# Group B's prompt attention from two streams of heads, their steps on part of the array in pairs; combine queued behind the heads

## The chip, the cores and the metric

The kernel runs on one NeuronCore of one Trainium2 chip. The metric is the device time of one execution in microseconds; the median of three runs is given, and one more execution was recorded by the profiler. Engines go by the profile's names: PE is TensorE (its weight loads are PEld), DVE VectorE, ACT ScalarE, POOL GpSimd, and SP the engine that issues most DMAs.

## What is computed

One layer of an encoder with two groups of attention heads beside each other, for a prompt of 512 frames and 8 x 16 frames of decoding, with 2048 channels in float32. The 640 frames share every projection.

```python
def prompt_layer(x, w_in, norm_mix, rel_table, sinks, norm_grp_a, norm_grp_b, w_out,
                 norm_ffn, w_gate, w_up, w_down):
    ...
    qa, ka, va, qb, kb, vb = split_proj(rmsnorm(x, norm_mix) @ w_in)
    qb = rope_partial(qb, pos)
    kb = rope_partial(kb, pos)
    ...
    oa = band_attend(qa.reshape(b, nc, CHUNK, N_HEADS_A, 1, HEAD_DIM),
                     band_gather(ka, A_PREV_CHUNKS), band_gather(va, A_PREV_CHUNKS),
                     band_valid(nc, A_PREV_CHUNKS), bias=bias)
    ob = band_attend(qb.reshape(b, nc, CHUNK, N_KV_B, GQA_R, HEAD_DIM),
                     band_gather(kb, B_PREV_CHUNKS), band_gather(vb, B_PREV_CHUNKS),
                     band_valid(nc, B_PREV_CHUNKS), sink=sinks.reshape(N_KV_B, GQA_R))
    y = merge_and_ffn(x, oa, ob, norm_grp_a, norm_grp_b, w_out, norm_ffn, w_gate, w_up, w_down)
    keep_a = min(A_REACH, s)
    keep_b = min(B_WINDOW, s)
    return y, ka[:, s - keep_a:], va[:, s - keep_a:], kb[:, s - keep_b:], vb[:, s - keep_b:]
```

`sample_layer` does the same for the decoding frames against cached keys and values. Group B has 16 query heads of 64 channels on two key and value heads, a window of its own chunk and two before, and a sink for each head.

## The kernel before

**Projections.** `dense` (L247) multiplies one tile of 128 weight columns by the 16 chunks of the input's channels. Each product of float32 is three matmuls (L235, L236, L237: high by high, high by low, low by high), for two halves of 320 frames: 16 x 2 x 3 = 96 matmuls of 128x320 a tile. The low parts come from a copy on ScalarE (L226) and a subtraction on VectorE (L227, `split`).

**Stages at the start.** First the keys and values of group B with the norm of the input. Then the eight query tiles of group B, `project_b` (two heads of one key head each; tile t), each followed by its rotation (`rope`, L555, through small DMAs) and a store of its decoding frames to the scratch tensor `sb_d` (L871). Then four tiles of group A, (1,7), (0,7), (2,6) and (2,7), each reduced by L410 or L412 and stored. Then group A's other tiles, two at a time, by a scheme with seven products instead of eight (`quartet`: p1, p6, p7, p2, p5, p4, p3; its weights are combined at L797, L801, L804 and L813, its results at L823), which needs sums of the input's chunks.

**Side work.** Attention and the sums are generators that wait in queues. A stream takes the generators of one queue in turn; `tick`, called after six projection matmuls, lets `pump` advance the next stream by one step, at a rate (`n.rate`, steps a tick). Here they are:
- `prompt_b`, one for each tile t, in the queue "heads": scores (L425) in two times two banks, masked maxima (L428), softmax (L436 to L445), four steps of transposes (L341, `flip`), and the weighing of the values (L464). Scores use 64 rows of TensorE's array (64*128 in the profile), weighings 64 columns (128*64).
- `decode_b` in "decode": loads, among them the query from `sb_d` (L584, copied at L590), then four steps of scores (L599), softmax (L612 to L616), transposes (L341) and products with the values (L651).
- `combine(k0, k1)` in "combine": for each chunk kt two loads of the input (L889, L890), sums on VectorE (L896, L903) and GpSimd (L897, L899), and three splits. Its two buffers of a chunk come from the few W buffers.

A step that uses part of the array is announced by `yield "part"`. Where two streams have such a step next, `pump` runs both (the partner's beside the first). Where no partner stands ready, a step is put off once, but before the change only with more than two streams. `drain` and `drain_queue` run what is left without projection matmuls between.

**Order and buffers.** The program is written in this order and then scheduled; `keep_pace` holds a side instruction on TensorE behind the projection matmul that it was written after. Scores, transposes and weighings share four banks of PSUM (`at`), projections two pairs (`dn`). There are 62 buffers S of 640 columns, 12 W of 1024 and some for the queries (Q). In the stage of `project_b` there was one stream of heads, and `combine(0, 3)` was queued with decode, behind the last `project_b`.

Of the kernel before, what the change touches and what calls it, by code (L numbers as in the profile page):

```python
# [49 lines left out]
class Net:  # L50
# [24 lines left out]
    def pump(self, alone=False):  # L75

        skipped = False
        for _ in range(len(self.streams)):
            name, queue = self.streams[self.turn % len(self.streams)]
            self.turn += 1  # L80
            work = self.active.get(name)
            if work is None and self.queues.get(queue):
                work = self.active[name] = self.queues[queue].pop(0)
            if work is None or work.gi_running:
                continue
            partner = None
            if self.marks.get(name) and not alone:
                partner = next((x for x, y in self.active.items() if x != name and y and self.marks.get(x)
                                and not y.gi_running), None)
                if partner is None and len(self.streams) > 2 and name not in self.waited:  # L90
                    self.waited.add(name)
                    skipped = True
                    continue
            at = self.emitted()
            self.run(name, work)
            if partner:
                self.run(partner, self.active[partner])
                self.due -= 1
            self.side.append((at, self.emitted()))
            return True  # L100
        return skipped and self.pump(alone)
# [218 lines left out]
def build(nc, tc, io, pools):  # L320
    n = Net(nc, tc, io, pools)
# [24 lines left out]
    def pack(t, k):  # L346
        v = r(sh(t, 2, k))
        return v[:, 0], v[:, 1]
# [56 lines left out]
    def proj(idx, lst, ps=None, gain=None):  # L405
        if ps is None:
            ps = n.dense([(io["w_in"][idx, :, k:k + 8], 8) for k in (0, 8)], acts)
        out = n.get(lst)
        if gain is None:
            nc.vector.tensor_tensor(halves(out[:, :TOK]), ps, halves(r_mix), ALU.mult)  # L410
        else:
            nc.vector.scalar_tensor_tensor(halves(out[:, :TOK]), ps, gain, halves(r_mix), ALU.mult, ALU.mult)  # L412
        return out
# [441 lines left out]
    qps.append(n.dense([(io["w_in"][27, :, k:k + 8], 8) for k in (0, 8)], acts))  # L855
    n.drain()
    n.rate = 0.55
    nc.vector.tensor_tensor(kb, kf, r_mix, ALU.mult)
    n.put("F", kf)
    rope(kb)  # L860
# [7 lines left out]
    def project_b(t):  # L868
        q = proj(26 + t, "Q", qps.pop(0) if qps else None, 0.125)
        rope(q)  # L870
        dma(out=sb_d[:, t], in_=q[:, SP:])  # L871
        heads_of(prompt_b, t, [("Q", q)], q)

    def keep_a(i, p, x):
        if i:
            dma(out=io["o_ka" if i == 1 else "o_va"][p], in_=x)
        dma(out=qkv_d[i, p], in_=x)
        n.put("S", x)
# [4 lines left out]
    def combine(k0, k1):  # L883

        tt, st = nc.gpsimd.tensor_tensor, nc.vector.scalar_tensor_tensor
        third = n.get("S" if k0 == 6 else "W")
        for kt in range(k0, k1):
            a, c = n.get("W"), n.get("W")
            dma(out=a[:, :TOK], in_=io["xT"][:, kt])  # L889
            dma(out=c[:, :TOK], in_=io["xT"][:, kt + 8])  # L890
            yield
            g = g_mix[:, kt + 8:kt + 9]
            a11, a21, a12, a22 = a[:, :HT], a[:, HT:TOK], c[:, :HT], c[:, HT:TOK]
            s1, s2 = a[:, TOK:TOK + HT], c[:, TOK:TOK + HT]
            nc.scalar.activation(a[:, :TOK], a[:, :TOK], AF.Identity, scale=g_mix[:, kt:kt + 1])
            st(s1, a22, g, a21, ALU.mult, ALU.add)  # L896
            tt(s2, s1, a11, ALU.subtract)  # L897
            s3 = third[:, HT * (kt % 3):HT * (kt % 3) + HT]
            tt(s3, a21, a11, ALU.subtract)  # L899
            thirds[kt] = third, s3  # L900
            for which, x in ((3, s1), (1, s2), (6, a12)):
                if which == 6:
                    st(a12, a12, g, s2, ALU.mult, ALU.subtract)  # L903
                t = n.get("S")
                sums[kt][which] = t, pack(t, HT)
                n.split(x, *sums[kt][which][1])
            n.put("W", a, c)
            yield
# [12 lines left out]
    for t in range(8):  # L921
        project_b(t)
        if t == 0:
            n.rate = 0.85
    n.put("S", cos, sin)
    n.streams = (("heads 0", "heads"), ("decode 0", "decode"), ("combine", "combine"))
    n.add("combine", combine(0, 3))
    n.add("decode", decode_b())
    n.rate = 1.25
    for i, p in ((1, 7), (0, 7), (2, 6), (2, 7)):  # L930
        keep_a(i, p, proj(8 * i + p, "S", None, None if i else 0.125))
        if (i, p) == (0, 7):
            n.drain_queue("heads")
            n.move("Q", "S", 4)
            n.add("combine", combine(3, 6))
    n.drain()

# [522 lines left out]
```

## Time and profile before

| | |
|---|---|
| median of 3 runs (lowest, highest) | 2529.17 us (2527.81, 2533.78) |
| the profiled execution's own time, its span | 2528.33 us, 2526.6 us |
| query tiles of B, tiles of A, first quartet | about 60 to 283 us of the span |
| last matmul of tile (2,7) starts, first quartet's first three products wait | about 276.5 us; 281.52 and 282.56 us |
| HBM read, written | 311.14 MB, 86.87 MB |

A row of the timeline has the start in us, the us that one took (of several, from the first's start to the last's end), the engine, the line, the operation, its output and inputs, and behind "x" how many stand together; in brackets stands the idle time of its engine just before it and what ended that.

### The profile page before, as it was taken

How to read it: one execution, taken by the hardware profiler on the slowest of the kernel's cores; microseconds unless marked ns; L12 is line 12 of the kernel's file. 1: busy time of each engine (PE TensorE's matmuls, PEld its weight loads, DVE VectorE, ACT ScalarE, POOL GpSimd, SP SyncE). 2: the span in 40 equal slices, each digit the busy share in tenths (PEclk: the TensorE clock that was granted, in tenths of full speed). 3: DMA queues.
4: the chain of work that ended last, by engine and by line, in shares of the span. 5: the costliest groups of instructions: out<-in, count | busy, mean ns of one | idle time of the engine just before them, and what ended most of it. 6: DMA issues, size and time to landing. Idle time of an engine off the chain costs nothing.

```text
span 2526.6 us, 44669 instructions
## 1 busy us (share of the span) xinstructions
PE 2484.5 (98%) x17325; PEld 2420.7 (96%) x17325; DVE 1965.5 (78%) x2930; ACT 1055.0 (42%) x1701; POOL 701.9 (28%) x566
## 2 busy tenths in 40 slices
PE   8999999999999999999999999999999999999997
PEld 8998999987799999999999999999999999999997
DVE  6657766685668887788888888888889877777797
ACT  5446333365555543343343343434434333333343
POOL 1001212110022043323333232333325433333453
PEclk9999999999999999999999999999999999999998
DMA  6233433478664434543344334334437756666655
GB/s 198 83 97 119 163 132 119 147 248 292 229 201 145 148 112 147 166 148 121 124 145 136 128 129 150 120 123 146 132 127 259 234 167 177 176 170 178 181 161 183
DMA packets 191605, 401.68 MB, mean 159 GB/s; under 512 B 22497, under 2 KB 83937, under 8 KB 191393
## 3 DMA queue, kind: packets, MB, share of 16 engines
q1 hardware_dynamic: 167056, 344.75, 41.8%
q0 software_dynamic: 23184, 52.77, 7.6%
q8 instruction: 136, 2.23, 0.4%
q10 hardware_dynamic: 1152, 1.31, 0.2%
q14 instruction: 77, 0.62, 0.1%
HBM read 311.14 MB, written 86.87 MB: 158 GB/s over the span
## 4 chain that ended last, share of the span: by engine, by line
PE 88%; DVE 7%; issue 2%; DMA 2%; ACT 1%; SPq 0%; POOL 0%; DVEq 0%; ACTq 0%; POOLq 0%
PE dn L235 18%; PE dn L237 18%; PE dn L236 17%; PE at L235 10%; PE at L237 10%; PE at L236 10%; DVE W L227 2%; PE at L341 2%; PE at L464 1%; PE at L425 1%; DVE S L823 1%; DMA W<-w_in 1%; PE at L743 0%; DMA W<-xT 0%; ACT S L438 0%
## 5 line engine op out<-in xcount | busy, mean ns | idle before, releaser
L226 ACT ACTIVATE W<-W 128x1024 fp32r<-128x1024 f32 (+2 forms) x662 | 640.3, 968 | 1064.3 <-PE dn L236 582.4
L235 PE MATMUL dn<-S,W 128*128 128x320 f32 x3374 | 1054.5, 313 | 7.4 <-ACT S L1159 3.8
L237 PE MATMUL dn<-S,W 128*128 128x320 f32 x3374 | 1045.8, 310 | 5.7 <-DVE W L227 5.4
L236 PE MATMUL dn<-S,W 128*128 128x320 f32 x3374 | 1044.2, 309 | 0.3 <-DVE S L227 0.3
L227 DVE TENSOR_TENSOR W<-W,W 128x1024 fp32r<-128x1024 f32 (+2 forms) x662 | 800.3, 1209 | 90.5 <-ACT W L226 83.2
L235 PEld LDWEIGHTS dn<-S,W 128*128 128x128 f32 x3374 | 634.3, 188 | 22.3 <-issue 13.5
L237 PEld LDWEIGHTS dn<-S,W 128*128 128x128 f32 x3374 | 633.6, 188 | 11.6 <-DVE W L227 9.9
L236 PEld LDWEIGHTS dn<-S,W 128*128 128x128 f32 x3374 | 634.4, 188 | 0.8 <-DVE S L227 0.6
L237 PE MATMUL at<-S,W 128*128 128x320 f32 x1834 | 567.8, 310 | 1.0 <-DVE W L227 1.0
L235 PE MATMUL at<-S,W 128*128 128x320 f32 x1834 | 567.9, 310 | 0.5 <-ACT W L226 0.5
L236 PE MATMUL at<-S,W 128*128 128x320 f32 x1834 | 567.7, 310 | 0.0
L804 POOL TENSOR_TENSOR W<-W,W 128x1024 f32<-128x1024 f32 (+2 forms) x84 | 181.4, 2159 | 772.9 <-DVE W L227 629.1
L237 PEld LDWEIGHTS at<-S,W 128*128 128x128 f32 x1834 | 345.1, 188 | 1.7 <-DVE W L227 1.4
L235 PEld LDWEIGHTS at<-S,W 128*128 128x128 f32 x1834 | 345.1, 188 | 0.7 <-ACT W L226 0.7
L236 PEld LDWEIGHTS at<-S,W 128*128 128x128 f32 x1834 | 345.1, 188 | 0.0
L823 DVE TENSOR_TENSOR S<-S,dn 128x320 f32<-128x320 f32 x398 | 182.5, 482 | 80.0 <-PE dn L237 79.7
L813 POOL TENSOR_TENSOR W<-W,W 128x1024 f32<-128x1024 f32 (+2 forms) x84 | 186.1, 2216 | 183.7 <-DVE W L227 132.8
L823 DVE TENSOR_TENSOR S<-S,at 128x320 f32<-128x320 f32 x292 | 138.6, 484 | 96.5 <-PE at L237 94.8
L797 DVE TENSOR_TENSOR W<-W,W 128x1024 f32<-128x1024 f32 (+2 forms) x86 | 117.4, 1365 | 40.8 <-DMA W<-w_gate 29.4
L801 DVE TENSOR_TENSOR W<-W,W 128x1024 f32<-128x1024 f32 (+2 forms) x86 | 95.9, 1115 | 55.1 <-DMA W<-w_up 29.6
L1112 POOL DMA_DIRECT2D S<-act_d x161 | 88.0, 547 | 166.5 <-PE dn L237 80.0
L1176 DVE TENSOR_TENSOR S<-S,half 128x320 fp32r<-128x320 f32 x147 | 120.3, 839 | 1.9
(157 smaller groups left out, 1700.4 us busy)
## 6 DMA issues: line engine op xcount, KB each, us to landing
S<-act_d POOLq DMA_DIRECT2D x161, 320.0 KB, 3.8
W<-w_gate SPq DMA_DIRECT2D x88, 512.0 KB
W<-w_up SPq DMA_DIRECT2D x88, 512.0 KB
W<-w_in SPq DMA_DIRECT2D x66, 512.0 KB
W<-w_down SPq DMA_DIRECT2D x64, 384.0 KB
act_d<-half SPq DMA_DIRECT2D x147, 160.0 KB
act_d<-S SPq DMA_DIRECT2D x147, 160.0 KB
W<-w_down SPq DMA_DIRECT2D x68, 320.0 KB
```

The source lines that it names most:

```text
L226: self.nc.scalar.activation(hi, src, AF.Identity)
L227: self.nc.vector.tensor_tensor(lo, src, f(hi), ALU.subtract)
L235: mm(out, a[0], b[0], start=first, stop=False)
L236: mm(out, a[0], b[1], start=False, stop=False)
L237: mm(out, a[1], b[0], start=False, stop=last)
L797: nc.vector.tensor_tensor(b12[:, w], b12[:, w], b22[:, w], sub)
L801: nc.vector.tensor_tensor(s6[:, w], b11[:, w], b12[:, w], sub)
L804: eng.tensor_tensor(b11[:, w], b22[:, w], s6[:, w], sub)
L813: eng.tensor_tensor(b21[:, w], b21[:, w], s6[:, w], sub)
L823: add = lambda o, a, b: nc.vector.tensor_tensor(o, a, b, ALU.add)
L1112: nc.gpsimd.dma_start(out=r(sh(t, 2, HT)), in_=r(act_d[which, :, j]))
L1176: nc.vector.tensor_tensor(r(src), src, hi, ALU.subtract)
```

## The change

Four edits: the stage of group B's query tiles has two streams of heads instead of one, and a step on part of the array is put off once from two streams on; the rate behind the first query tile is 0.9 instead of 0.85; decode and combine are added to the two streams of heads; and `combine(0, 3)` is queued where `combine(3, 6)` is, after the queue of heads has been emptied beside the tile (0,7).

```diff
--- before.py
+++ after.py
@@ -87,7 +87,7 @@
             if self.marks.get(name) and not alone:
                 partner = next((x for x, y in self.active.items() if x != name and y and self.marks.get(x)
                                 and not y.gi_running), None)
-                if partner is None and len(self.streams) > 2 and name not in self.waited:
+                if partner is None and len(self.streams) > 1 and name not in self.waited:
                     self.waited.add(name)
                     skipped = True
                     continue
@@ -855,6 +855,7 @@
     qps.append(n.dense([(io["w_in"][27, :, k:k + 8], 8) for k in (0, 8)], acts))
     n.drain()
     n.rate = 0.55
+    n.streams = (("heads 0", "heads"), ("heads 1", "heads"))
     nc.vector.tensor_tensor(kb, kf, r_mix, ALU.mult)
     n.put("F", kf)
     rope(kb)
@@ -921,10 +922,9 @@
     for t in range(8):
         project_b(t)
         if t == 0:
-            n.rate = 0.85
+            n.rate = 0.9
     n.put("S", cos, sin)
-    n.streams = (("heads 0", "heads"), ("decode 0", "decode"), ("combine", "combine"))
-    n.add("combine", combine(0, 3))
+    n.streams += (("decode 0", "decode"), ("combine", "combine"))
     n.add("decode", decode_b())
     n.rate = 1.25
     for i, p in ((1, 7), (0, 7), (2, 6), (2, 7)):
@@ -932,6 +932,7 @@
         if (i, p) == (0, 7):
             n.drain_queue("heads")
             n.move("Q", "S", 4)
+            n.add("combine", combine(0, 3))
             n.add("combine", combine(3, 6))
     n.drain()
 
```

What moves is seen best in each engine's instructions in order. A name like S_224_1430 is a buffer (S, number 224 given out) and a count of names; dn, at are banks. First TensorE, in the middle of the query tiles. Before, scores (L425) and a weighing (L464) of two tiles have projection matmuls on both sides; the weighing there:

```order
L236 MATMUL dn_1441<-S_47_168,W_237_1523 128x320
L237 MATMUL dn_1441<-S_46_167,W_238_1524 128x320
L464 MATMUL at_1534<-S_229_1471,S_5_83 64x256
L464 MATMUL at_1534<-S_233_1496,S_5_83 64x256
...
L464 MATMUL at_1534<-S_231_1483,S_5_83 64x128
L464 MATMUL at_1534<-S_235_1514,S_5_83 64x128
L235 MATMUL dn_1441<-S_49_173,W_237_1523 128x320
```

In the changed kernel a block of scores stands directly ahead of the weighing of an earlier tile (the block's middle is left out):

```order
L235 MATMUL dn_1442<-S_40_155,W_228_1444 128x320
L425 MATMUL at_1522<-S_4_82,S_224_1430 128x128
...
L425 MATMUL at_1532<-S_4_82,S_224_1430 128x256
L425 MATMUL at_1533<-S_4_82,S_224_1430 128x256
L464 MATMUL at_1542<-S_221_1416,S_5_83 64x256
L464 MATMUL at_1542<-S_233_1484,S_5_83 64x256
...
L464 MATMUL at_1542<-S_241_1508,S_5_83 64x128
L236 MATMUL dn_1442<-S_41_156,W_228_1444 128x320
```

So one return to projections between the two is gone here; there are two such places, and one with two weighings together. Next TensorE at decode's first scores, behind the last query tile. Before, they (L599) stand ahead of the scores of query tile 7 (L425, with the query S_333_2094):

```order
L237 MATMUL dn_2439<-S_16_105,W_413_2442 128x320
L599 MATMUL at_2200<-S_345_2137,S_347_2139 128x144
L599 MATMUL at_2201<-S_345_2137,S_347_2139 128x144
L599 MATMUL at_2200<-S_345_2137,S_347_2139 128x144
L599 MATMUL at_2201<-S_345_2137,S_347_2139 128x144
L425 MATMUL at_2349<-S_4_82,S_333_2094 128x128
L425 MATMUL at_2350<-S_4_82,S_333_2094 128x128
L425 MATMUL at_2349<-S_4_82,S_333_2094 128x256
L425 MATMUL at_2350<-S_4_82,S_333_2094 128x256
L235 MATMUL dn_2439<-S_16_105,W_412_2441 128x320
```

Now tile 7's scores (the query S_337_2112) come first, and 26 projection matmuls lie between their last and decode's first:

```order
L425 MATMUL at_2176<-S_4_82,S_337_2112 128x256
L236 MATMUL dn_2124<-S_59_192,W_387_2312 128x320
L237 MATMUL dn_2124<-S_58_191,W_388_2313 128x320
...
L236 MATMUL dn_2124<-S_71_216,W_387_2312 128x320
L237 MATMUL dn_2124<-S_70_215,W_388_2313 128x320
L599 MATMUL at_2185<-S_350_2150,S_352_2152 128x144
L599 MATMUL at_2186<-S_350_2150,S_352_2152 128x144
L599 MATMUL at_2185<-S_350_2150,S_352_2152 128x144
L599 MATMUL at_2186<-S_350_2150,S_352_2152 128x144
L235 MATMUL dn_2479<-S_10_93,W_423_2481 128x320
```

Decode's scores stand at the seam between two projection tiles now. Last VectorE, at the end of the four tiles of A, where the reduction of the last tile (L410) and the weights of the first two quartets (L797, L801, L227 into W) meet. Before:

```order
L801 TENSOR_TENSOR W_546_3177<-W_545_3174,W_543_3170 128x1024
L227 TENSOR_TENSOR W_548_3180<-W_545_3174,W_547_3179 128x1024
L227 TENSOR_TENSOR S_41_156<-S_521_2990,S_40_155 128x320
L797 TENSOR_TENSOR W_569_3416<-W_569_3416,W_570_3418 128x1024
L410 TENSOR_TENSOR S_540_3164<-dn_3055,S_1_79 128x640
L227 TENSOR_TENSOR W_551_3219<-W_546_3177,W_550_3218 128x1024
L227 TENSOR_TENSOR W_555_3258<-W_543_3170,W_554_3257 128x1024
L801 TENSOR_TENSOR W_572_3423<-W_571_3420,W_569_3416 128x1024
```

In the changed kernel (L897 and L904 are the two sums of combine on VectorE, L896 and L903 before the change's added line):

```order
L904 SCALAR_TENSOR_TENSOR W_517_2973<-W_517_2973,gains 128x320
L227 TENSOR_TENSOR S_519_2989<-W_517_2973,S_519_2989 128x320
...
L410 TENSOR_TENSOR S_540_3164<-dn_3041,S_1_79 128x640
L227 TENSOR_TENSOR W_551_3219<-W_546_3177,W_550_3218 128x1024
L227 TENSOR_TENSOR S_38_150<-S_521_3008,S_37_149 128x320
L897 SCALAR_TENSOR_TENSOR W_527_3033<-W_528_3034,gains,W_527_3033 128x320
L227 TENSOR_TENSOR S_41_156<-S_521_3008,S_40_155 128x320
L227 TENSOR_TENSOR S_534_3058<-W_527_3033,S_534_3058 128x320
L904 SCALAR_TENSOR_TENSOR W_528_3034<-W_528_3034,gains 128x320
L227 TENSOR_TENSOR S_535_3061<-W_528_3034,S_535_3061 128x320
L227 TENSOR_TENSOR W_555_3258<-W_543_3170,W_554_3257 128x1024
```

The L797 with the second quartet's weights (W_569) has gone behind the L410, and combine's last two chunks (W_517, then W_527 and W_528) stand around it.

## Prediction

> **What bounds the kernel now.** I read the page's shares and chain first. Columns of the second row: busy us, share of the span, instructions; the third row is the chain by engine.
>
> ```profile
> span 2526.6 us, 44669 instructions
> ...
> PE 2484.5 (98%) x17325; PEld 2420.7 (96%) x17325; DVE 1965.5 (78%) x2930; ACT 1055.0 (42%) x1701; POOL 701.9 (28%) x566
> ...
> PE 88%; DVE 7%; issue 2%; DMA 2%; ACT 1%; SPq 0%; POOL 0%; DVEq 0%; ACTq 0%; POOLq 0%
> ```
>
> TensorE is busy in 2484.5 of 2526.6 us and carries 88% of the chain. The change alters no arithmetic, so it can win only what TensorE waits or loses at switches where its order changes: group B's query tiles and the four tiles of A behind them, 60 to 283 us. All of TensorE's waits there (who waited for whom: us in total, times, longest):
>
> ```profile
> PE dn L235 <- DVE S L410: 1.1, 1, 1.1
> PE at L425 <- ACT S L612: 0.9, 1, 0.9
> PE at L341 <- DVE S L445: 0.8, 1, 0.8
> PE dn L237 <- DVE W L227: 0.5, 1, 0.5
> PE at L341 <- DVE S L616: 0.5, 2, 0.3
> ```
>
> Together 3.8 us, 0.15% of the span. Better cover can win no more than this, and one half-speed stretch (1.7 us, below).
>
> **The sum is made against the profiled execution**, 2528.33 us by its own time (span 2526.6, so 1.7 around it). The median of the runs is 2529.17, 0.84 higher; I add the differences to the median.
>
> **Two streams and pairs.** The edit wants one visit to part of the array where two tiles' steps made two. The price of a visit, from a block of scores between projection matmuls (start us, us, instruction):
>
> ```profile
> 110.78 0.31 PE L236 MATMUL dn<-S,W 128*128 128x320 f32 x1
> 110.93 0.31 PE L237 MATMUL dn<-S,W 128*128 128x320 f32 x1
> 111.17 1.79 PE L425 MATMUL at<-S,S 64*128 64x128 f32 x16
> 112.88 0.41 PE L235 MATMUL dn<-S,W 128*128 128x320 f32 x1
> 113.13 0.31 PE L236 MATMUL dn<-S,W 128*128 128x320 f32 x1
> ```
>
> Projection matmuls start 0.15 us apart; into the block it is 0.24, and 0.25 after the first one behind it. [...] So 0.2 to 0.3 us a visit, and I take 0.3. If the sixteen visits of group B became eight, that would be 8 x 0.3 = 2.4 us. In the order they do not. Counting runs of scores, weighings and decode products with nothing else between, this stretch holds 24 visits before and 25 now: one block of scores takes all four banks, so a second tile's scores start only some 15 matmuls later, two scores stand against a weighing and one pair of weighings is merged, while decode's blocks come apart. That is **+0.3**. Group A's attention, much later, has 28 visits before and 26 now, because the turn of the streams starts elsewhere: **-0.6**.
>
> Even a merged visit need not save a whole one, where scores (64*128) meet a weighing (128*64). Products with values (L651) before scores (L599), and before a projection matmul:
>
> ```profile
> 235.37 1.09 PE L651 MATMUL at<-S,S 128*64 128x128 f32 x16
> 236.40 0.76 PE L599 MATMUL at<-S,S 64*128 64x144 f32 x8
> ...
> 257.08 1.09 PE L651 MATMUL at<-S,S 128*64 128x128 f32 x16
> 258.11 0.41 PE L235 MATMUL dn<-S,W 128*128 128x320 f32 x1
> ```
>
> The next instruction starts 1.03 us behind the block either way, so the step from one use of the part to the other costs as much as the step back to projections: such a pair has three switches where two visits have four, and saves about 0.1 us.
>
> [...]
>
> Where a block is followed at once by work on the same four banks, TensorE may wait for VectorE's reads. VectorE's reads of such a block (start, us):
>
> ```profile
> 112.12 0.29 DVE L428 CUSTOM_DVE_ANT_0 S<-at,cst 128x128 f32<-128x128 f32 x1 [7.45 <-PE at L425]
> ...
> 112.34 0.42 DVE L428 CUSTOM_DVE_ANT_0 S<-at,cst 128x256 f32<-128x256 f32 x1
> ```
>
> The first bank is free at 112.76, the block ends at 112.88, so a weighing behind it waits for nothing if VectorE is idle. Tile 3's scores are followed by 11 transposes through the next banks. Two reads free a bank in 0.64 us (112.12 to 112.76), three or four transposes take 0.45 to 0.6 at 0.15 each: 0.1 a bank, so I take **+0.4** for four, with 0 and 2 as bounds for all such places.
>
> **The rate 0.9 for 0.85** has no price of its own: it moves the same steps a few projection matmuls (0.15 us each) earlier, under TensorE's own work.
>
> **Waits that go.** Combine's chunk 2 runs beside the heads of the last tiles before the change, and VectorE and then TensorE stop there:
>
> ```profile
> 190.02 0.55 DVE L903 SCALAR_TENSOR_TENSOR W<-W,gains 128x320 f32<-128x320 f32 x1 [1.06 <-POOL W L897]
> ...
> 191.50 0.33 PE L341 MATMUL at<-cst,S 128*128 128x128 f32 x1 [0.83 <-DVE S L445]
> ```
>
> With combine queued behind tile 7, nothing in VectorE's queue stands ahead of that softmax: **-0.8**. Then the 0.90 in tile 7's scores, and the clock behind it (windows: stretch, its us, then busy us of TensorE, its loads, VectorE, ScalarE, GpSimd, then granted clock, DMA share, GB/s):
>
> ```profile
> 216.61 1.13 PE L425 MATMUL at<-S,S 64*128 64x256 f32 x4 [0.90 <-ACT S L612]
> ...
> 219.10:222.40 3.30, 3.30 (x19) 2.97 (x20) 1.72 (x10) 1.55 (x3) 0.20 (x1) 0.50 0.01 2
> 222.50:225.90 3.40, 3.40 (x33) 3.08 (x30) 2.36 (x11) 3.12 (x14) 0.41 (x2) 1.00 0.66 213
> ```
>
> Those scores waited for a bank that the exponentials of decode's first scores (L612) still read; now they stand 26 projection matmuls ahead of decode's, so **-0.9**. For 3.3 us behind it the clock was 0.50, 19 matmuls against 33 in a stretch as long: about half of it, 1.7 us, is lost. With the wait and the blocks around it pulled apart I take this off too, **-1.7**; it is the least sure term, since a wait of 1.21 us elsewhere left the clock at 1.00:
>
> ```profile
> 541.58 0.70 PE L425 MATMUL at<-S,S 64*128 64x256 f32 x3 [1.21 <-DVE sm L428]
> ...
> 541.60:546.00 4.40, 4.40 (x29) 4.06 (x30) 4.17 (x17) 1.19 (x5) 0.21 (x1) 1.00 1.01 371
> ```
>
> [...]
>
> **Waits that come.** (1) Decode's first scores need tile 7's query, through DRAM. The chain before:
>
> ```profile
> 202.62 0.82 DVE L563 TENSOR_TENSOR S<-S,S 80x640 f32<-80x640 f32 x1
> 203.35 1.23 SPq L890 DMA_DIRECT2D W<-xT  x1
> 204.67 0.38 SPq L871 DMA_DIRECT2D sb_d<-S  x1
> 207.48 1.33 SPq L584 DMA_DIRECT2D S<-sb_d  x2
> 211.68 0.61 POOL L590 COPY S<-S 128x512 f32<-128x512 f32 x1 [2.85 <-DMA S<-sb_d]
> 212.49 0.76 PE L599 MATMUL at<-S,S 64*128 64x144 f32 x8
> ```
>
> From the rope's end (203.44) to the scores are 9.05 us; without combine's load (1.23) in SP's queue, about 7.8. TensorE has, between tile 7's own scores and decode's, 1.8 us for those scores and 26 projection matmuls of 0.15, 3.9: 5.7. So it waits 2.1 us if tile 7's scores start at once, and nothing if they start 2.1 us behind the rope; I take **+0.6**, bounds 0 and 2.1. Behind decode's score in TensorE's queue stand all later matmuls.
>
> (2) Combine's chunks 2 and 3 now lie between 212 and 281. VectorE there (same columns):
>
> ```profile
> 212.00:257.00 45.00, 43.58 (x315) 36.87 (x314) 36.96 (x152) 30.15 (x96) 8.70 (x18) 0.96 0.33 107
> 257.00:281.00 24.00, 23.42 (x168) 22.85 (x166) 16.81 (x28) 10.26 (x20) 6.23 (x5) 1.00 0.72 232
> ...
> 240.00:257.00 17.00, 16.49 (x115) 14.04 (x113) 16.48 (x54) 12.67 (x36) 4.09 (x4) 1.00 0.52 162
> ...
> 276.79 0.49 DVE L227 TENSOR_TENSOR S<-S,S 128x320 fp32r<-128x320 f32 x1
> ```
>
> It has 69 - 36.96 - 16.81 = 15.2 us free. Two chunks bring six splits of 0.49 and four of 0.55 (L903's row), 5.1 us, and two waits of 1.06 for GpSimd: 7.3. They fit in all, but not from 240 to 257 (16.48 of 17.00), so some split of weights or copy for decode comes late: **+0.5**, bounds 0 and 3.
>
> (3) The first quartet. Before, it paid 1.10 + 0.51, because the reduction of the last tile (L410) stood behind a wait for weights:
>
> ```profile
> 278.63 2.01 DVE L797 TENSOR_TENSOR W<-W,W 128x1024 f32<-128x1024 f32 x1 [1.35 <-DMA W<-w_in]
> ...
> 281.52 0.39 PE L235 MATMUL dn<-S,W 128*128 128x320 f32 x1 [1.10 <-DVE S L410]
> ...
> 282.56 0.41 PE L237 MATMUL dn<-S,W 128*128 128x320 f32 x1 [0.51 <-DVE W L227]
> ```
>
> Now L410 stands ahead of that L797, but behind combine's chunk 6, and chunk 7 (its two W slots reused, so load, GpSimd and VectorE in series: the store's issue 204.67 to the copy at 211.68 shows that two transfers with a wait take 7.0 us, one 3.5) stands behind it, with the split that the second product needs. Bounds: both old waits go, -1.6; one load's 3.5 comes out in full, +3.5 less what goes. I take **+1.0**.
>
> **Sum**: +0.3 -0.6 +0.4 -0.8 -0.9 -1.7 +0.6 +0.5 +1.0 = -1.2, so 2527.1 for the profiled execution's own time and **2528.0** against the median.
>
> **The rivals.**
> - *The pairs merge on the chip as named*: 2.4 us for eight visits instead of my +0.3, that is 2525.3. For it speaks the price of a visit; against it the order, where the visits stand apart. The change then does what it says; in the likeliest case it does not.
> - *The half-speed stretch stays*, or moves to another crowd of short blocks: 2528.0 + 1.7 = 2529.7, no change at all. For it speaks that the trace had it after only 0.90 us of waiting, so that something besides the wait may cause it; against it the same blocks later with a clock of 1.00 at 541.60.
> - *The first quartet waits for one whole load more*: 2528.0 + 3.5 - 1.0 = 2530.5. For it speaks that two slots serve chunks 5, 6 and 7 in turn; against it the 3.6 us of the first product that hide most of it (24 matmuls of 0.15).
> - *Slower: VectorE's queue fills* from 240 to 281. Its place is the split of weights (L227) behind combine's rows; if 7.3 us of new work meet less than 7.3 us of room ahead of a weight that TensorE needs, all the rest lands on TensorE. It decides when the work falls wholly between 240 and 257 with 0.5 us of room: 6.8 us late, with the last load's 3.5 behind it 10.3 less the 1.5 already in the sum: 2528.0 + 8.8 = 2536.8. Against it speaks that 7.2 us of room follow from 257 on, and 8.0 lie ahead of 257.
>
> **How the numbers follow.** My forecast 0.70; half-speed stays 0.15; pairs merge 0.05; quartet 0.05; VectorE's queue 0.05. With every unknown at its lower bound (no rotation, no new wait, both old waits of the quartet gone) the sum is -1.2 -0.4 -0.6 -0.5 -2.6 = -5.3, and with the merged pairs' 2.4 it is -7.7: 2521.5. With rotation, decode's chain and VectorE at their upper bounds and the clock's stretch kept it is -1.2 +1.6 +1.5 +2.5 +1.7 = +6.1: 2535.3. So the range is 2521.5 to 2535.5. A measurement of this kernel tells about 0.3%, 7.6 us, from no change. Waits and half clock together are 5.5 us, less than that, so faster has only 0.03; slower, the last rival, 0.05; within 0.3%, 0.92.
>
> **What would show it.** Right: no wait of L425 for L612 and no half clock near 216 to 222; no 0.83 wait of L341; 25 visits, none saved; decode's first scores waiting up to 2 us for GpSimd's copy; the first quartet waiting for a split of combine's chunk 7. Wrong: a median under 2521.5, which would need TensorE to lose time somewhere that its waits don't show; or VectorE at full load from 240 to 281 with L227 ending TensorE's waits, above 2535.5.

## The result

| | before | changed |
|---|---|---|
| median, lowest to highest (6 runs each) | 2528.53 us, 2527.73 to 2534.23 | 2541.51 us, 2538.02 to 2543.42 |
| ratio, 95% interval | | 1.0046, 1.0035 to 1.0056 |

The changed kernel is slower by 13 us, 0.46%, outside the range of the prediction. Its profiled execution, 14.9 us longer in span than the one before (2541.5 against 2526.6), is the slowest of the six (2543.42 us), so its trace shows about 2 us more than the medians do. The page's first rows and the chain by engine:

```profile
span 2541.5 us, 44642 instructions
...
PE 2488.3 (98%) x17325; PEld 2425.9 (95%) x17325; DVE 1970.6 (78%) x2930; ACT 1054.8 (42%) x1701; POOL 702.7 (28%) x566
...
PE 86%; DVE 7%; DMA 3%; ACT 2%; issue 1%; POOL 0%; SPq 0%; DVEq 0%; ACTq 0%; POOLq 0%
```

TensorE does the same matmuls and is busy 3.8 us longer (matmuls at half clock count as busy: 6.50 of the 6.65 us from 551.95 on, below); the rest of the 14.9 us is waiting. TensorE's waits from 60 us to the end of the first quartet's trouble, 306 us (for whom, us, times, longest):

```profile
PE dn L235 <- DVE S L410: 4.6, 1, 4.6
PE at L599 <- POOL S L590: 1.9, 1, 1.9
PE dn L237 <- DVE W L227: 1.5, 2, 1.4
PE at L341 <- DVE S L445: 1.2, 2, 1.0
PE at L237 <- DVE W L227: 0.6, 1, 0.6
PE at L651 <- ACT S L642: 0.6, 1, 0.6
PE at L425 <- DVE S L563: 0.6, 1, 0.6
```

The wait for the exponentials (L612) is gone, the one for the last tile's reduction (L410) has grown from 1.1 to 4.6 (the quartet's second product, p6, writes the pair of banks that L410 reads), and decode's scores (L599) wait 1.9. Where the time was lost shows best if the same projection matmul is looked up in both traces. The last matmul of the first quartet's p1 starts at 280.11 before, the quartet's last one, 144 matmuls later, at 303.34 (rows of before):

```profile
280.11 0.31 PE L237 MATMUL dn<-S,W 128*128 128x320 f32 x1
...
303.34 0.31 PE L237 MATMUL dn<-S,W 128*128 128x320 f32 x1
```

The same two in the changed kernel:

```profile
279.84 0.31 PE L237 MATMUL dn<-S,W 128*128 128x320 f32 x1
284.73 0.60 PE L235 MATMUL dn<-S,W 128*128 128x320 f32 x1 [4.58 <-DVE S L410]
...
311.69 0.31 PE L237 MATMUL dn<-S,W 128*128 128x320 f32 x1
```

Up to 280 us, through all query tiles, decode and the four tiles of A, the changed kernel is 0.27 us *ahead*, less than the 1.2 us by which two traces of the kernel before differ there (table below). The rest of the first quartet takes 31.85 us instead of 23.23, **8.6 us** more. The next such step lies between the 2881st and the 4609th projection matmul of the trace, around group A's attention: 364.0 us instead of 359.5, **4.6 us** more. The stretches between and behind them differ by 0.6 and 1.5 us.

The granted clock fell in both places. The windows where it fell there in the changed kernel, with the stretch that had it before in the first row (stretch, us, busy us of TensorE, its loads, VectorE, ScalarE, GpSimd, granted clock, DMA share, GB/s):

```profile
219.10:222.40 3.30, 3.30 (x24) 3.07 (x24) 3.23 (x18) 2.36 (x10) 0.00 (x0) 1.00 0.35 131
282.30:289.10 6.80, 4.20 (x14) 3.83 (x15) 4.77 (x9) 3.18 (x6) 1.26 (x2) 0.50 0.86 263
551.95:558.60 6.65, 6.50 (x24) 5.81 (x25) 4.36 (x22) 2.98 (x10) 0.21 (x1) 0.50 1.00 367
```

The half clock near 219 is gone, as forecast, but two others have come, each twice as long, the first behind the 4.6 us of waiting. At 0.50 the projection matmuls start 0.27 us apart (554.42, 554.69, 554.95), at 1.00 0.15 (289.30, 289.44, 289.59), so about 45% of TensorE's busy time there is lost, an estimate of 1.9 us of the first (4.20 busy) and 2.9 of the second (6.50).

Why L410 comes late is read from VectorE and GpSimd ahead of it, in the changed kernel. VectorE first:

```profile
276.53 1.17 DVE L897 SCALAR_TENSOR_TENSOR W<-W,gains,W 128x320 f32<-128x320 f32 x1
277.62 4.16 DVE L227 TENSOR_TENSOR S<-W,S 128x320 fp32r<-128x320 f32 x3
281.70 0.54 DVE L904 SCALAR_TENSOR_TENSOR W<-W,gains 128x320 f32<-128x320 f32 x1
282.17 1.68 DVE L227 TENSOR_TENSOR S<-W,S 128x320 fp32r<-128x320 f32 x4
283.77 0.81 DVE L410 TENSOR_TENSOR S<-dn,S 128x640 f32<-128x640 f32 x1
```

GpSimd beside it:

```profile
276.10 1.24 POOL L900 TENSOR_TENSOR W<-W 128x320 f32<-128x320 f32 x1 [7.26 <-ACT W L896]
277.31 2.66 POOL L804 TENSOR_TENSOR W<-W,W 128x1024 f32<-128x1024 f32 x1
279.93 1.10 POOL L898 TENSOR_TENSOR W<-W 128x320 f32<-128x320 f32 x1
```

L410 could have run from about 276.7 on, when the last tile's matmuls were done (p1's 24 of 0.147 us start behind them). VectorE was not idle. It worked in the order of its queue through combine's rows: the sums and splits of one chunk, and splits of the third sums (s3) of several. That chunk is not chunk 6, as the prediction has it: chunks 6 and 7 put their third sum into an S buffer, and L900 at 276.10 writes W. In the program's order it is chunk 5. Four of the splits take 0.4 us each at the end (1.68 for four); the first of the three at 277.62 takes as long as GpSimd's L804 beside it:

```profile
277.62 2.70 DVE L227 TENSOR_TENSOR S<-W,S 128x320 fp32r<-128x320 f32 x1
```

GpSimd's queue holds the same chunk up. L904 needs the sum that L898 makes, and L898 stands behind L804 and ends at 281.03. So a short split alone would have let L904 start at most about 0.7 us earlier than 281.70.

### The profile page after: what moved, and what is told of

Same layout as the page of the kernel before. It is cut to its first block, busy times and chain, and to the rows that moved or that the text cites. A ratio compares the mean times of both kernels' runs of the same rounds, so it can differ in the third digit from the quotient of the medians.

```text
span 2541.5 us, 44642 instructions
## 1 busy us (share of the span) xinstructions
PE 2488.3 (98%) x17325; PEld 2425.9 (95%) x17325; DVE 1970.6 (78%) x2930; ACT 1054.8 (42%) x1701; POOL 702.7 (28%) x566
## 4 chain that ended last, share of the span: by engine, by line
PE 86%; DVE 7%; DMA 3%; ACT 2%; issue 1%; POOL 0%; SPq 0%; DVEq 0%; ACTq 0%; POOLq 0%
PE dn L235 17%; PE dn L237 17%; PE dn L236 17%; PE at L237 10%; PE at L235 10%; PE at L236 10%; DVE W L227 2%; PE at L341 2%; DMA W<-w_in 1%; PE at L464 1%; PE at L425 1%; DVE S L428 1%; DVE S L823 1%; ACT S L438 1%; DVE S L227 0%
## 5 line engine op out<-in xcount | busy, mean ns | idle before, releaser
L226 ACT ACTIVATE W<-W 128x1024 fp32r<-128x1024 f32 (+2 forms) x662 | 640.2, 968 | 1085.3 <-PE dn L236 570.0
L227 DVE TENSOR_TENSOR W<-W,W 128x1024 fp32r<-128x1024 f32 (+2 forms) x662 | 797.6, 1205 | 87.4 <-ACT W L226 83.2
L804 POOL TENSOR_TENSOR W<-W,W 128x1024 f32<-128x1024 f32 (+2 forms) x84 | 181.5, 2161 | 767.2 <-DVE W L227 608.9
L797 DVE TENSOR_TENSOR W<-W,W 128x1024 f32<-128x1024 f32 (+2 forms) x86 | 119.4, 1388 | 39.7 <-DMA W<-w_gate 28.8
L801 DVE TENSOR_TENSOR W<-W,W 128x1024 f32<-128x1024 f32 (+2 forms) x86 | 95.9, 1115 | 58.5 <-DMA W<-w_up 30.8
```

The source lines that it names most:

```text
L226: self.nc.scalar.activation(hi, src, AF.Identity)
L227: self.nc.vector.tensor_tensor(lo, src, f(hi), ALU.subtract)
L797: nc.vector.tensor_tensor(b12[:, w], b12[:, w], b22[:, w], sub)
L801: nc.vector.tensor_tensor(s6[:, w], b11[:, w], b12[:, w], sub)
L804: eng.tensor_tensor(b11[:, w], b22[:, w], s6[:, w], sub)
```

## The experiments

Each kernel's run is timed beside runs of the kernel before. Kernels whose name begins with a_ start from the changed kernel, those with b_ from the one before. The positions of the same matmuls as above, in each profiled execution:

| | p1's last, us | from there to the quartet's last | group A's stretch | ratio to before (95%) |
|---|---|---|---|---|
| before | 280.11 | 23.23 | 359.5 | |
| again (before, once more) | 281.30 | 22.74 | 359.2 | |
| changed | 279.84 | 31.85 | 364.0 | 1.0046 (1.0035, 1.0056) |
| a_turn | 280.13 | 30.53 | 360.6 | 1.0042 (1.0029, 1.0054) |
| b_turn | 280.42 | 22.55 | 360.0 | 1.0009 (1.0000, 1.0018) |
| b_combine | 292.29 | 21.11 | 361.0 | 1.0041 (1.0029, 1.0054) |
| a_fill (24 matmuls more) | 280.05 | 33.65 | 362.3 | 1.0050 (1.0037, 1.0064) |
| a_early17 | 281.42 | 25.41 | 359.1 | 1.0012 (1.0003, 1.0020) |
| a_p2 | 278.83 | 35.26 | 359.7 | 1.0057 (1.0043, 1.0071) |
| a_port | 279.99 | 33.01 | 362.4 | 1.0046 (1.0028, 1.0063) |
| a_rate | 280.43 | 32.15 | 360.7 | 1.0034 (1.0021, 1.0047) |
| b_early17 | 287.01 | 22.49 | 360.9 | 1.0019 (1.0010, 1.0028) |
| a_early17_p2 | 283.77 | 25.46 | 360.7 | 1.0022 (1.0013, 1.0031) |
| b_p2 | 280.31 | 22.45 | 359.2 | 1.0002 (0.9993, 1.0012) |

The kernels before and again are one program. So, as shown below, are a_turn and a_rate in the order of every engine. Two traces of one order thus differ by 0.3 to 1.2 us at p1's last matmul, by 0.5 to 1.6 in the rest of the quartet and by 0.1 to 0.3 in group A's stretch.

### Group A's attention: the state that is carried over

The edit to the early stage changes where the turn of the streams stands when group A's attention starts. One line sets that state; with it, every engine's order behind that point is that of the other kernel. a_turn:

```diff
             n.streams = (("heads 0", "heads"), ("decode 0", "decode"), ("heads 1", "heads"), ("decode 1", "decode"))
+            n.turn, n.due, n.active = 327, 0.6, dict.fromkeys(("heads 0", "combine", "decode 0"))
```

> The changed kernel with the state of the scheduler (the turn of the streams, the fraction of a step that is due, the order in which partners are looked for) set, where group A's attention begins, to what it is there in the kernel before; from there on every engine's order is that of before. Theory 1 (the carried state alone costs the 5 us that the trace shows between 520 and 770 us: waits of 0.63 and 1.60 us for L428 and 6.9 us at half clock): 2541.5 - 5 = 2536.5 us, no half clock near 550, waits of TensorE there as before (2.1 us for L428). Theory 2 (something left by the earlier stage, buffers or transfers, costs it): 2541.5, half clock near 550 stays.

b_turn sets 452, 0.4 and the order of the changed kernel in the kernel before.

> The kernel before with only that state set to what it is in the changed kernel. Theory 1: 2528.5 + 5 = 2533.5 us, with a half-speed stretch of 6 to 7 us near 542 to 550. Theory 2: 2528.5, no such stretch.

a_turn took 2540.12 us, b_turn 2532.56 (before 2529.72 in these rounds): neither theory as stated. a_turn has the waits of before (2.1 us for L428) and its stretch is 3.4 us shorter than the changed kernel's, yet still has a half clock (0.57 from 552 to 556); b_turn, with the changed kernel's order and waits there, has none:

```profile
540.00:560.00 20.00, 17.77 (x135) 15.95 (x134) 13.69 (x53) 14.63 (x41) 0.42 (x2) 1.00 0.65 225
```

Without a half clock the changed order takes 360.0 (b_turn), 359.7 (a_p2) or 362.3 us (a_fill) against 359.1 to 359.5, so by these traces the state itself costs **0.2 to 3.2 us**. (b_turn's trace is of an execution of 2528.93 us, below the median of 2532.56; what the others lost is not traced.) The rest of the changed kernel's 364.0, 1.7 to 4.3 us, goes with the half-speed stretch near 552, which this order had in one trace of five (changed; not b_turn, a_fill, a_p2, nor a_port, which had one near 750), and the order of before in five of nine (a_turn, b_combine, a_rate, b_early17, a_early17_p2, whose stretches take 360.6 to 361.0 us; not before, again, b_p2, a_early17, with 359.1 to 359.5).

The kernel before, once more, asks the same of the stretch near 219:

> The kernel before once more, unchanged, for a second trace. Theory 6 (the half-speed stretch behind a short wait comes by chance of its time, so that the -1.7 of the prediction was no property of the order): the waits near 191, 216 and 281 us are the same to 0.3 us, the half clock near 219 to 222 is missing or elsewhere. Rival (the order sets it): 3.4 us at 0.50 at the same place.

2529.04 us, and the rival: its half clock was there again (0.79 on the mean), behind a wait of 0.8 us for L612.

```profile
216.00:224.00 8.00, 7.18 (x42) 5.29 (x40) 6.04 (x39) 3.52 (x12) 0.33 (x2) 0.79 0.02 6
```

But in b_turn and b_p2, whose order up to there is the same and whose TensorE waits 1.0 us for L612, it was not; b_turn:

```profile
216.00:224.00 8.00, 7.04 (x53) 5.19 (x52) 6.96 (x40) 4.07 (x16) 0.61 (x3) 1.00 0.18 66
```

So in two traces of four. The order makes such a stretch possible; whether it comes is not settled by the order alone. The waits ahead of it do not settle it either: it came behind 0.8 and 0.9 us (again, before) and not behind 1.0 (b_turn, b_p2), in all four beside blocks on part of the array. What does is not shown.

### The first quartet: combine alone, and where it is queued

b_combine moves only combine, with one stream of heads (and the state of before at group A):

```diff
-    n.add("combine", combine(0, 3))
     n.add("decode", decode_b())
...
             n.move("Q", "S", 4)
+            n.add("combine", combine(0, 3))
             n.add("combine", combine(3, 6))
```

> The kernel before with combine(0,3) queued where combine(3,6) is, one stream of heads as before, and the same state as before at group A's attention. Theory 3 (combine's rows ahead of L410 in VectorE's queue cost the first quartet its 8.6 us): about 2528.5 - 0.8 (the wait at 191) + 8 = 2535 to 2537, TensorE waiting 3 to 5 us for L410 and a half-speed stretch behind it. Rival (the two streams of heads push the steps so late that they meet there): 2528, wait for L410 at most 1.5 us.

2538.74 us: **this edit alone makes the kernel as slow as all four** (the intervals, 1.0029 to 1.0054 and 1.0035 to 1.0056, overlap). The place of the wait was missed: it is not L410 but the first weights of the quartet, and p1 itself ends 12.2 us late. So the loss is shown to come from combine's place; its path from there to TensorE differs between the two kernels.

```profile
285.46 0.64 PE L235 MATMUL dn<-S,W 128*128 128x320 f32 x1 [7.95 <-ACT W L226]
```

a_early17 queues combine(0,3) one tile of A earlier, with the state of before at group A (at its old place, two streams of heads leave no free S buffer):

```diff
+        if (i, p) == (1, 7):
+            n.add("combine", combine(0, 3))
         if (i, p) == (0, 7):
             n.drain_queue("heads")
             n.move("Q", "S", 4)
-            n.add("combine", combine(0, 3))
             n.add("combine", combine(3, 6))
```

> The changed kernel with combine(0,3) queued one tile of A earlier, beside (0,7), and the state at group A's attention as before. Theory 3 (combine's last chunks end too late for the first quartet): with 16 ticks more for them the quartet's wait falls from 4.6 to at most 1.5 us, without half clock behind it: 2540.1 (the run with the state alone) - 6 = 2534. Rival (the two streams of heads cause the quartet's loss, wherever combine is queued): 2540, a wait of 3 us or more.

2533.36 us, 6.8 below a_turn as expected (6) and 5.0 below a_rate, with a wait of 1.74 for L410, a little more than expected, and a half clock behind it (0.69 from 284 to 288). SP's rows show what moved. Loads of combine (xT) and of the quartet's weights (w_in) in the changed kernel:

```profile
264.69 4.91 SPq L783 DMA_DIRECT2D W<-w_in  x2
270.14 0.33 SPq L890 DMA_DIRECT2D W<-xT  x1
270.92 0.33 SPq L891 DMA_DIRECT2D W<-xT  x1
280.35 0.33 SPq L783 DMA_DIRECT2D W<-w_in  x1
281.86 0.33 SPq L890 DMA_DIRECT2D W<-xT  x1
283.48 0.33 SPq L891 DMA_DIRECT2D W<-xT  x1
283.89 0.38 SPq L783 DMA_DIRECT2D W<-w_in  x1
```

In a_early17 the last load of combine:

```profile
268.30 0.81 SPq L783 DMA_DIRECT2D W<-w_in  x2
269.61 0.33 SPq L891 DMA_DIRECT2D W<-xT  x1
270.03 12.92 SPq L783 DMA_DIRECT2D W<-w_in  x4
```

and in the kernel before:

```profile
259.79 0.34 SPq L783 DMA_DIRECT2D W<-w_in  x1
265.11 0.33 SPq L890 DMA_DIRECT2D W<-xT  x1
...
266.85 5.37 SPq L783 DMA_DIRECT2D W<-w_in  x4
```

Chunk 7's last load is issued at 283.5 us in the changed kernel, at 269.6 in a_early17 and at 265.1 before. The quartet's further weights, which stand behind it in SP's queue, move with it. What decides is which chunk takes the W buffer that decode's output leaves. SP's wait for the store of that output (ob_d), before and then changed:

```profile
SPq L890 <- DMA ob_d<-W: 4.9, 1, 4.9
```

```profile
SPq L891 <- DMA ob_d<-W: 3.0, 1, 3.0
```

Before, this wait ends with chunk 7's last load at 265.11, and in a_early17 again with chunk 7's (269.61). In the changed kernel it ends with chunk 3's second load, at 263.37. In the program's order chunk 5 and then chunk 7 follow through that same buffer, each load (270.92, 283.48) behind the last split of the chunk before.

b_early17 is a_early17 without the two streams, the putting off and the rate:

```diff
-    n.add("combine", combine(0, 3))
     n.add("decode", decode_b())
...
+        if (i, p) == (1, 7):
+            n.add("combine", combine(0, 3))
```

> The kernel before, one stream of heads, with combine(0,3) queued where the run a_early17 queues it, and the same state at group A's attention; against a_early17 (2533.4) it differs in the two streams, the putting off and the rate alone. Theory 7 (the two streams cost or save at most 2 us, the rest of the 3.5 us left in a_early17 is combine's one tile of delay): 2532 to 2535. Rival (the two streams themselves cost the 3.5 us): 2530, the stretch from 60 to 277 us 1 us shorter than in a_early17.

2534.96 us, 1.0019 against 1.0012 with overlapping intervals: the two streams cost nothing that can be seen. Here p1 ends 5.6 us later than in a_early17 (287.01 against 281.42), and the rest of the quartet takes 2.9 us less. What the delayed combine costs sits elsewhere here, in VectorE's queue for decode's softmax:

```profile
248.56 0.50 PE L341 MATMUL at<-cst,S 128*128 128x128 f32 x2 [3.63 <-DVE S L616]
```

### What the late chunks collide with

a_rate raises the rate of steps behind (0,7):

```diff
             n.add("combine", combine(3, 6))
+            n.rate = 1.7
```

> The changed kernel with 1.7 instead of 1.25 steps a tick behind the tile (0,7), and the state at group A's attention as before. Theory 3a (combine ends too late because its steps are issued too slowly): wait for L410 at most 1.5 us, 2540.1 - 6 = 2534. Theory 3b (its chunks take their turns at the same few W buffers, each behind the load and the sums of the one before, whatever the rate): the wait stays within 1 us of 3.5, 2540.

2538.34 us, with a wait for L410 of 4.5, at the edge of 3b's bound and far from 3a's 1.5. Chunk 7's loads are issued at 282.36 and 283.98. But the edit reached nothing: in the trace the instructions of every engine stand in a_turn's order (only some S buffers are others). So the rate is not what sets combine's order here, and a_rate is a_turn once more; what really faster steps would do is not shown. That the chunks wait for their buffers rests on the rows above: SP's load at 283.48 comes just behind the split that ends at 283.45 and reads that buffer.

a_port gives GpSimd's sums of the first quartet's weights to VectorE (the first of the two then stands behind p7):

```diff
-        for _, y in collect(quartet(8, load, sums, split_thirds if at == 0 else None, release if last else None)):
+        for _, y in collect(quartet(8, load, sums, split_thirds if at == 0 else None, release if last else None, eng=nc.gpsimd if at else nc.vector)):
```

> The changed kernel with the first quartet's sums of weights that GpSimd makes (L804, L813) made by VectorE. Theory 5 (a VectorE operation beside one of GpSimd lasts as long as that one: L227 took 2.70 us beside L804's 2.66, L897 1.17 beside L900's 1.24): chunk 6's L227 take 0.48 us, L410 comes 2.2 us earlier, TensorE's wait for it is 2.4 us: about 2539. Rival (the 2.70 us are a wait of its own, whatever GpSimd does): 2.70 and 4.6 us stay, 2541.5 or more.

The same split, no longer beside L804, and L410:

```profile
277.48 0.48 DVE L227 TENSOR_TENSOR S<-W,S 128x320 fp32r<-128x320 f32 x1
...
281.44 0.81 DVE L410 TENSOR_TENSOR S<-dn,S 128x640 f32<-128x640 f32 x1
```

0.48 instead of 2.70, and L410 2.3 us earlier (281.44 against 283.77). So the split's 2.70 was GpSimd's doing. The 2.3 us are not the split's alone, since L898 no longer stands behind L804 either (it starts at 277.69 instead of 279.93); no run separates the two. The time did not follow: 2542.75 us, since the quartet then waited for chunk 7:

```profile
282.40 0.39 PE L235 MATMUL dn<-S,W 128*128 128x320 f32 x1 [2.10 <-DVE S L410]
...
291.18 0.63 PE L235 MATMUL dn<-S,W 128*128 128x320 f32 x1 [3.38 <-ACT S L226]
```

a_fill computes the first quartet's p1 twice (the second time over the first, so 24 matmuls more):

```diff
-            for j in range(k):
+            for j in [*range(k)] * (2 if lefts is sums and before and which == 0 else 1):
```

> The changed kernel with the first product (p1) of the first quartet computed twice, 24 more matmuls of 0.147 us = 3.5 us, which lie in TensorE's wait of 4.6 us for L410. Theory 4 (the half clock behind that wait comes from the idle time, and costs some 2.2 us): the clock stays at 1.00 from 280 to 292, wait for L410 about 1.1 us, 2541.5 - 2.2 = 2539.3. Rival (the half clock has another cause): half clock stays, 2541.5 or more.

The clock stayed at 1.00 from 280 to 288, but at 289.47 TensorE waited 1.78 us for chunk 7, the half clock came behind that wait, and the time was 2541.87, not 2539.3:

```profile
280.00:288.00 8.00, 7.21 (x48) 6.69 (x46) 5.75 (x12) 3.31 (x6) 0.95 (x2) 1.00 0.85 264
288.00:297.00 9.00, 6.05 (x20) 5.03 (x21) 4.90 (x7) 3.56 (x6) 0.91 (x1) 0.62 0.41 144
```

The half clock came behind the waiting again; covering one wait with work only uncovered the next.

a_p2 moves the product p2 ahead of p6 (its result is added once p6's is formed):

```diff
         yield "p1", product(b11, 0, x[:, 0])
+        early = lefts is sums and before
+        if early:
+            b21 = get(2)
+            yield "p2", product(b21, 4, n.bank()[:, :HT])
...
-        b21 = get(2)
-        if part == "all":
+        b21 = b21 if early else get(2)
+        if part == "all" and not early:
             yield "p2", product(b21, 4, n.bank()[:, :HT])
```

> The changed kernel with the first quartet's product p2, which needs neither the last tile's bank nor combine's sums, moved ahead of p6: 24 matmuls, 3.5 us, lie in the wait. Theory 3: the wait for L410 falls from 4.6 to about 1.1 us, no half clock behind it, 2541.5 - 3.5 - 2.2 = 2535.8. Rival (the sums of chunk 7 are as late and take the place of L410): the wait moves to a split of chunk 7, 2540 to 2541.

The rival, and worse: 2545.75 us (the profiled execution, 2540.48 us, is the fastest of the six). ScalarE's copy of p6's weights (L226 into W) stands in ScalarE's queue behind chunk 7's copies, which wait for chunk 7's load. TensorE, then ScalarE in this run (L904 there is the line that is L896 in the changed kernel):

```profile
288.60 0.64 PE L235 MATMUL dn<-S,W 128*128 128x320 f32 x1 [9.46 <-ACT W L226]
```

```profile
283.34 0.83 ACT L904 ACTIVATE W<-W,gains 128x640 f32<-128x640 f32 x1 [2.25 <-DMA W<-xT]
...
287.51 1.04 ACT L226 ACTIVATE W<-W 128x1024 fp32r<-128x1024 f32 x1
```

Two more asked whether p2's move helps where chunk 7 is in time:

> a_early17 with the first quartet's p2 ahead of p6 as well. With combine's chunk 7 in time the 24 matmuls cover the wait of 1.74 and 0.52 us and the half clock behind it: 2533.4 - 2.3 - 1.7 = 2529.4. Rival (the weights or sums of p6 come as late as in a_p2): 2533 or more.

> The kernel before with p2 ahead of p6 in the first quartet. If only waits of TensorE count, it saves the 1.10 + 0.51 us there: 2528.3, not to be told from 2529.9 by the interval. Rival (VectorE's rows for chunk 7 now behind L410 come late, as in a_p2): a wait for ACT's split of p6's weights of 3 us or more, 2533.

a_early17_p2 took 2534.62 us: the wait for L410 is gone, one of 1.58 for p2's own weights (ACT W L226) stands in its place, and no gain is left. b_p2 took 2529.69 against 2529.82: its quartet waits 1.07 once instead of 1.10 and 0.51, no difference that can be told. No version beat the kernel before.

## Why the prediction was wrong

- **The step that failed is the first quartet**, "(3)" among the waits that come: "+1.0", with bounds of -1.6 and +3.5. It measured +8.6. The kind of wait was named (L410 behind a chunk of combine, chunk 7's split behind that); its size was not, and the chunk ahead of L410 was 5 and not 6. Four things were left out. Chunk 7 was priced as one load, while chunks 3, 5 and 7 pass through one W buffer in series in the changed kernel, so that chunk 7's last load came 18.4 us later (283.5 instead of 265.1). GpSimd's queue was not followed: chunk 5's sum L898 stood behind L804 until 279.93. VectorE's rows were priced at 0.49 and 0.55 each, while beside GpSimd one took 2.70; the row of L797 with 2.01 us, quoted in the prediction, showed such a row already: 0.93 of it lie beside GpSimd's L804 (277.01 to 279.56 in the trace of before), and an L797 of the same size takes 1.22 with GpSimd idle (changed kernel, 271.65). And a longer wait can bring a half-speed stretch (0.50 for 6.80 us behind the 4.58), which was a term where it went but not where it might come. A bound of "one load in full" was no bound for a chain through four queues.
- **The range** was narrower than its own terms. Its upper sum leaves out the quartet's own bound, 2.5 us more than the value taken (2537.8 with it), and the slower rival's 2536.8 lies above its end. The measured 2541.5 lies above both.
- **The slower rival** (VectorE's queue fills, splits come late, 2536.8 us) had the nearest kind of cause and about 60% of the size (7.6 of 13.0 us), at a chance of 0.05. Its test, 7.3 us of work against the room in 240 to 257, asked about VectorE's total; what decided was that combine's chain ends behind the quartet's start.
- **Query tiles, decode and tiles of A**: forecast -1.6 us without quartet and group A (+0.3 +0.4 -0.8 -0.9 -1.7 +0.6 +0.5), measured -0.3 at p1's last matmul, within the 1.2 us between two traces of one kernel. By step: the 0.90 wait for L612 went, as said. The 0.83 wait for L445 did not: TensorE still waits 0.97 at 190.53, with combine gone from VectorE's queue; the chain there runs from the scores at 183.18 to the divided row at 190.48, and a split of projection weights (L227, 183.70 to 184.93) now stands ahead of the maxima in VectorE's queue, which the prediction took to be empty. Decode's first scores waited 1.9 us, inside the bounds of 0 to 2.1, three times the value taken; the order before had this wait too in some traces (none in before, 1.4 in again). Of the 0.3 us a visit, which the +0.3 and the -0.6 rest on, the rows show 0.19 (0.24 and 0.25 where 0.15 is usual) and no run shows the rest; the gain of a pair is too small to show, and no run has tested it by itself; that visits hardly merge is read from the order alone.
- **The half clock** near 219, "-1.7", was absent in the changed kernel's trace, but is present in only two of four traces of the old order, so the term was worth about half of it.
- **Group A's attention**: forecast -0.6 for two visits fewer, measured +4.6 in the profile. 0.2 to 3.2 us of that come with the order, so the sign of the term was wrong too; the remainder goes with the half-speed stretch near 552, which that order has not had in four other traces.
- The sum of the runs: combine's place costs 5 to 9 us (a_turn 2540.1 and a_rate 2538.3 against a_early17 2533.4, and b_combine 9.0 above before); the carried state 1 to 3 (a_turn 1.4 below the changed kernel, intervals overlapping; b_turn 2.8 above before, its interval beginning at 1.0000); two streams and putting off none that can be seen. What makes up the 3.5 us that a_early17 still has over before, beside a wait of 1.7 for L410, 1.6 for decode's scores and one half-speed stretch, was not taken apart further.

## What to carry over

When side work is queued later, follow its last piece, not its total: through its buffers, its loads, and every engine's queue it shares, to the first main step behind it. Room on the busiest engine says nothing if the chain ends too late. And a wait on TensorE is priced with the half-speed stretch that may follow it, at the chance that traces show, in both signs: here 0.50 for 3.30 us behind a wait of 0.90 (before), for 6.80 behind 4.58 (changed kernel), and no half clock behind 1.0 (b_turn, b_p2).

## What was unexpected of the hardware

- A VectorE subtraction of 128x320 takes 0.48 us with GpSimd idle (changed kernel, 290.45) and 2.70 beside a GpSimd sum of 2.66 us (277.62); with that sum moved to VectorE it takes 0.48 (a_port, 277.48).
- Half-speed stretches (0.50) lasted 3.3 (before) and 6.8 and 6.65 us (changed kernel) by their windows. From the mean clock of 4 us windows they are estimated at about 3.4 us (a_early17: 0.69, 0.88) or 6.8 (a_turn: 0.80, 0.50, 0.85), and at 10.2 and 13.7 behind the longest waits (b_combine, 7.95: 0.70, 0.50, 0.52; a_p2, 9.46: 0.69, 0.50, 0.50, 0.60). One of about 3.3 us came behind waits of 0.8 and 0.9 us in two traces, and none behind the same wait of 1.0 us in two other traces of the same order.
